# A norm's sum of squares at the head of four layers: other engine, other priority

## The chip, the cores and the metric

One core of a Trainium2 chip runs the whole program. The metric is device time in microseconds, the median of the timed runs. Engines: TensorE (PE, matrix products; PEld, its weight loads), VectorE (DVE), ScalarE (ACT), GpSimd (POOL), and SyncE (SP), which issues most transfers. Engines run beside each other, each takes its own instructions in a fixed order, and semaphores tie them together.

## The reference

The input is 256 tokens of 1024 features. A first block (attention, delta rule, mixture of experts) is followed by a second block of four layers. Only the second block is touched by the change. Cut to what matters:

```python
def rms_norm_2(x, gain):
    y = x * lax.rsqrt(jnp.mean(x * x, axis=-1, keepdims=True) + RMS_EPS) * gain
    return y

for i in range(4):                       # mixers: stick-breaking, conv, gla, stick-breaking
    xn = rms_norm_2(h, norm_gains[i, 0])           # the norm of this document: the mixer's own
    m = mixer(xn, ...)                             # begins with xn @ w_in
    h = h + rms_norm_2(m, norm_gains[i, 1])
    f = squared_relu_mlp(rms_norm_2(h, norm_gains[i, 2]), ffn_w_up[i], ffn_w_down[i])
    h = h + rms_norm_2(f, norm_gains[i, 3])
```

## The kernel before

The residual stream lies transposed in `hT`: eight tiles of 128 features by 256 tokens (all fp32). Weights arrive as 1 MB pieces (`raw`), and `split` (L178) makes two parts of each 128x1024 half: `hi` on ScalarE (L190) and the rest `lo` on VectorE or, for the splits listed in `pool_lo`, on GpSimd (L193). The parts lie in `hi`/`lo`, `mg` or `split` by turns.

A mixer's first product works on `gain * hT`, and the factor `r = rsqrt(mean(hT**2) + eps)`, which belongs to a token and so to a column, is multiplied in later, when a product's result is taken out of PSUM. `operand` (L346) makes the two parts `xh` (ScalarE, L348) and `xl` (VectorE, L349) of `gain * hT` for each of the eight tiles. `chunk` (L221) runs 24 matmuls for 128 output features: `hi` and `lo` against `xh` (L228, L229), then `hi` against `xl` (L231). Its PSUM tile has the tag `g` or `s` by turns, with two buffers each; four chunks can be open before one has to be evacuated. The evacuation (`ev_q`, `ev_k` L676 to L681 in stick-breaking; `ev_c` L514 in conv; `ev_a` L763 in gla) multiplies by `r`.

`r` comes from `factor()` inside `pre` (L363), called by the first evacuation, so in the program it stands behind the first chunk's matmuls. It calls `sumsq` (L314): each hT tile is squared on ScalarE (L324) into `sq` (three buffers; the first of a summed group goes into `ss`); the first `8 - direct` squares are added up in `ss` (L331) by the engine given, and the rest, with `ss`, go through products with a matrix of ones (L337), which add over the partitions into a PSUM tile of tag `s`. Then `Net.factor` (L285) takes logarithm and exponential on ScalarE (L290, L291) and four steps on VectorE (L294 to L297, the last gives `r`).

What comes before: `post` (L380) at the end of a feed-forward layer normalizes its result (three of the eight products `mg` on GpSimd, L395; the others `mh` on VectorE, L398), adds it to hT (L401) and makes the operands tile by tile; `final` (L412) does the same after the first block (L431, L433). Both hold back the splits of the coming weights: four (`post`) or one (`final`) go ahead of the last operand, the others behind it. After `post` splits six and seven of the mixer are subtracted on GpSimd (`pool_lo`).

The order of instructions on each engine comes from a scheduler at build time that takes, among those it holds to be ready, the one with the best priority; priority is the place in the program. `high_priority(offset=50)` moves what it encloses 50 places ahead. The second sum of each layer (`ffn=True`) already uses GpSimd for six squares without that context; it is not changed.

Of the kernel before, what the change touches and what calls it, by code (L numbers as in the profile page):

```python
# [22 lines left out]
D = 1024  # L23
KD = D // P
# [52 lines left out]
class Net:  # L77
# [274 lines left out]
    def pre(self, gain, ffn=False, ops=None):  # L352


        nc = self.nc
        if ops is None:
            ops = self.operands()
            for k in range(KD):
                self.operand(k, gain, *ops)
        xh, xl = ops  # L360
        got = []

        def factor():  # L363
            if not got:
                r = self.nt("r", 2)
                got.append(r)
                if not ffn:
                    with self.tc.high_priority(offset=50):
                        ps = self.sumsq([self.hT[:, k] for k in range(KD)], nc.gpsimd, direct=8)
                        self.factor(ps, D, r)  # L370
                else:
                    ps = self.sumsq([self.hT[:, k] for k in range(KD)], nc.gpsimd, tag="g")
                    v = self.nt("fv", 1)
                    nc.vector.tensor_scalar(out=v, in0=ps, scalar1=1.0 / D, scalar2=EPS, op0=ALU.mult, op1=ALU.add)
                    nc.vector.scalar_tensor_tensor(out=r, in0=v, scalar=8.0 * EPS, in1=v, op0=ALU.mult, op1=ALU.mult)
            return got[0]

        return ([xh[:, k] for k in range(KD)], [xl[:, k] for k in range(KD)]), factor
# [1521 lines left out]
```

## Time and profile before

| | us |
|---|---|
| median of three timed runs | 1939.7 (1937.45 to 1941.39) |
| profiled execution, its own time | 1946.89 |
| its span, first to last instruction | 1945.1 |
| TensorE busy | 1865.7 |
| VectorE busy | 1118.4 |
| ScalarE busy | 952.8 |
| GpSimd busy | 152.5 |

The mean granted clock of TensorE is 0.986 of full speed. Times in the rows below count from the span's start. The four places of the change are the heads of the layers: stick-breaking at about 650 us, conv at 975, gla at 1271, stick-breaking at 1613. A matmul's record overlaps the next, so spacing tells its cost better than its length. A row with "x4" covers four instructions merged into one piece of the timeline, from the first start to the last end; what stands in brackets is the idle time of the engine before it and what ended it.

### The profile page before, as it was taken

Reading aid. Unit: us, or ns where it says so; the run is one execution under the profiler, and the core shown is the slowest. Engines: PE = TensorE matmul, PEld = TensorE weight load, DVE = VectorE, ACT = ScalarE, POOL = GpSimd, SP = SyncE. Lnnn points to the kernel's source line nnn. Section 1 sums busy time; section 2 is a strip of 40 time slices with the busy share of each in tenths; the row PEclk is TensorE's granted clock in tenths of the full one; section 3 lists DMA queues with packets and bytes.
Section 4 is the critical chain, followed back from the end, with each engine's and each line's share of the span. In section 5 each row is a group of like instructions: output and inputs, shape, how many; then the busy total and the mean of one; then the engine's idle time right before and its main releaser. Section 6 shows DMA issues by size and latency. Waiting matters only on the chain.

```text
span 1945.1 us, 34973 instructions
## 1 busy us (share of the span) xinstructions
PE 1865.7 (96%) x14445; PEld 1685.9 (87%) x14445; DVE 1118.4 (57%) x1955; ACT 952.8 (49%) x1742; POOL 152.5 (8%) x162
## 2 busy tenths in 40 slices
PE   6899998998999999999999999989999999999998
PEld 3787788765666899999999999979999998989998
DVE  4848447533332754755586755577675557556554
ACT  4535456322222674544444544455664446645443
POOL 2212111100000000100021100011010001000000
PEclk9999999999999999999999999999999999999999
DMA  9544276588999434455545455523445553335551
GB/s 328 193 152 154 90 239 246 210 324 342 406 399 346 131 130 152 152 174 190 178 145 194 153 183 185 194 87 109 152 152 175 191 177 124 115 131 176 175 192 44
DMA packets 196745, 369.19 MB, mean 190 GB/s; under 512 B 9189, under 2 KB 152997, under 8 KB 185061
## 3 DMA queue, kind: packets, MB, share of 16 engines
q1 hardware_dynamic: 193248, 362.77, 53.5%
q10 hardware_dynamic: 2900, 3.29, 0.5%
q8 instruction: 115, 1.88, 0.4%
q0 software_dynamic: 432, 0.84, 0.2%
q14 instruction: 50, 0.40, 0.1%
HBM read 364.25 MB, written 2.63 MB: 189 GB/s over the span
## 4 chain that ended last, share of the span: by engine, by line
PE 68%; DVE 4%; ACT 3%; POOL 1%; issue 1%; POOLq 0%; DVEq 0%; ACTq 0%
PE g L228 7%; PE g L231 7%; PE g L229 7%; PE big L216 7%; PE big L218 7%; PE big L217 7%; PE g L1761 4%; PE s L1801 2%; PE s L231 2%; PE s L228 2%; PE s L229 2%; PE s L218 1%; PE s L217 1%; PE s L216 1%; POOL ss L331 1%
## 5 line engine op out<-in xcount | busy, mean ns | idle before, releaser
L193 DVE TENSOR_TENSOR lo<-raw,hi 128x1024 fp32r<-128x1024 f32 x304 | 374.8, 1236 | 287.4 <-ACT hi L190 279.8
L190 ACT CAST hi<-raw 128x1024 fp32r<-128x1024 f32 x318 | 330.4, 1043 | 222.1 <-PE s L217 126.3
L228 PE MATMUL g<-xh,hi 128*128 128x256 f32 x1088 | 280.4, 292 | 16.0 <-ACT xh L348 5.6
L229 PE MATMUL g<-xh,lo 128*128 128x256 f32 x1088 | 276.6, 288 | 0.7 <-DVE lo L193 0.7
L228 PEld LDWEIGHTS g<-xh,hi 128*128 128x128 f32 x1088 | 211.2, 194 | 28.2 <-issue 8.4
L229 PEld LDWEIGHTS g<-xh,lo 128*128 128x128 f32 x1088 | 211.5, 194 | 2.2 <-DVE lo L193 0.9
L216 PE MATMUL big<-yh,hi 128*128 128x256 f32 x728 | 206.5, 284 | 0.0
L218 PE MATMUL big<-yh,lo 128*128 128x256 f32 x728 | 206.0, 283 | 0.0
L217 PE MATMUL big<-yl,hi 128*128 128x256 f32 x728 | 206.0, 283 | 0.0
L231 PE MATMUL g<-xl,hi 128*128 128x256 f32 x1088 | 156.7, 286 | 0.0
L231 PEld LDWEIGHTS g<-xl,hi 128*128 128x128 f32 x1088 | 142.7, 194 | 0.4 <-issue 0.2
L216 PEld LDWEIGHTS big<-yh,hi 128*128 128x128 f32 x728 | 139.7, 192 | 0.4 <-issue 0.3
L217 PEld LDWEIGHTS big<-yl,hi 128*128 128x128 f32 x728 | 139.7, 192 | 0.0
L218 PEld LDWEIGHTS big<-yh,lo 128*128 128x128 f32 x728 | 139.7, 192 | 0.0
L449 ACT ACTIVATE sq<-g 128x256 f32<-128x256 f32 x116 | 44.4, 383 | 173.1 <-PE g L231 173.1
L193 DVE TENSOR_TENSOR split<-raw,split 128x1024 fp32r<-128x1024 f32 x64 | 78.3, 1223 | 63.2 <-ACT split L190 63.2
L193 DVE TENSOR_TENSOR mg<-raw,mg 128x1024 fp32r<-128x1024 f32 x64 | 78.2, 1222 | 59.8 <-ACT mg L190 59.7
L190 ACT CAST split<-raw 128x1024 fp32r<-128x1024 f32 x64 | 66.8, 1044 | 63.8 <-PE s L218 42.8
L190 ACT CAST mg<-raw 128x1024 fp32r<-128x1024 f32 x64 | 66.8, 1043 | 51.6 <-PE s L218 36.2
L228 PE MATMUL s<-xh,hi 128*128 128x256 f32 x320 | 85.2, 296 | 5.7 <-DVE fv L294 2.5
L229 PE MATMUL s<-xh,lo 128*128 128x256 f32 x320 | 83.7, 292 | 0.7 <-DVE lo L193 0.7
L271 DVE TENSOR_TENSOR yl<-s,yh 128x256 fp32r<-128x256 f32 x76 | 32.1, 423 | 87.7 <-ACT yh L270 81.3
(613 smaller groups left out, 4665.8 us busy)
## 6 DMA issues: line engine op xcount, KB each, us to landing
raw<-in_ffn_w_up_dram SPq DMA_DIRECT2D x64, 1024.0 KB, 5.4
raw<-in_ffn_w_down_dram SPq DMA_DIRECT2D x64, 1024.0 KB, 5.0
raw<-in_w_mod_dram SPq DMA_DIRECT2D x24, 1024.0 KB, 6.7
raw<-in_sb_w_qkv_dram SPq DMA_DIRECT2D x24, 1024.0 KB, 5.3
raw<-in_w_in_dram SPq DMA_DIRECT2D x22, 1024.0 KB, 7.7
raw<-in_conv_w_in_dram SPq DMA_DIRECT2D x12, 1024.0 KB, 5.3
raw<-in_gla_w_in_dram SPq DMA_DIRECT2D x12, 1024.0 KB, 5.3
extra<-in_w_e_gate_dram SPq DMA_DIRECT2D x11, 1024.0 KB, 9.0
```

The lines of the kernel that those rows point to most:

```text
L190: i = nc.scalar.copy(hi, piece)
L193: j = on.tensor_tensor(out=lo, in0=piece, in1=hi.bitcast(F32), op=ALU.subtract)
L216: a = mm(out, whi, xhi, start=first, stop=False, skip_group_check=skip)
L217: mm(out, whi, xlo, start=False, stop=False, skip_group_check=skip)
L218: mm(out, wlo, xhi, start=False, stop=last, skip_group_check=skip)
L228: mm(ps, hi[:, k, sl], xh[k], start=k == 0, stop=False)
L229: mm(ps, lo[:, k, sl], xh[k], start=False, stop=False)
L231: mm(ps, hi[:, k, sl], xl[k], start=False, stop=k == kn - 1)
L271: self.nc.vector.tensor_tensor(out=lo, in0=src, in1=hi.bitcast(F32), op=ALU.subtract)
L449: nc.scalar.activation(out=t, in_=ps, func=AF.Relu)
L1761: on(mm(gu[i][64 * j:64 * j + 64, :], xg[:, k, o0 + j * cap:o0 + (j + 1) * cap], W[j][k], start=k == 0, stop=k == KD - 1, skip_group_check ...
L1801: on(mm(yps[64 * j:64 * j + 64, :], aT[:, f * P + 64 * j:f * P + 64 * j + 64], W[j][f][:, half * 512:half * 512 + 512], start=f == 0, stop ...
```

## The change

The call of `sumsq` in the mixers' own norm loses its `high_priority` context and its `direct=8`. With the default `direct=2`, six squares are added in `ss` by GpSimd (five additions), and `ss` and the last two squares go through products with ones: three in place of eight. The factor's steps keep their text, and lose the 50 places too. All four mixers use this function.

```diff
                 if not ffn:
-                    with self.tc.high_priority(offset=50):
-                        ps = self.sumsq([self.hT[:, k] for k in range(KD)], nc.gpsimd, direct=8)
-                        self.factor(ps, D, r)
+                    ps = self.sumsq([self.hT[:, k] for k in range(KD)], nc.gpsimd)
+                    self.factor(ps, D, r)
                 else:
```

## Rows read from the trace of the kernel before

**Rows 1.** The page's first part: busy time, share of the span, instructions.
```profile
PE 1865.7 (96%) x14445; PEld 1685.9 (87%) x14445; DVE 1118.4 (57%) x1955; ACT 952.8 (49%) x1742; POOL 152.5 (8%) x162
```

**Rows 2.** TensorE's waits, whole span: us in total, times, longest.
```profile
PE g L228 <- DVE glal L763: 5.2, 1, 5.2
...
PE big L696 <- DVE sbk L681: 1.5, 1, 1.5
...
PE g L228 <- DVE cc L514: 0.6, 1, 0.6
```

**Rows 3.** Timeline of ScalarE, head of conv: start, us, engine, line, operation.
```profile
981.22 0.42 ACT L324 ACTIVATE sq<-hT 128x256 f32<-128x256 f32 x1 [0.27 <-DVE hT L401]
...
982.25 0.49 ACT L348 ACTIVATE xh<-hT,vec_128c 128x256 fp32r<-128x256 f32 x1
982.65 1.03 ACT L190 CAST hi<-raw 128x1024 fp32r<-128x1024 f32 x1
983.59 0.47 ACT L290 ACTIVATE fy<-s,eps 128x256 f32<-128x256 f32 x1
```

**Rows 4.** Timelines of GpSimd and VectorE, conv, behind the operands.
```profile
985.07 4.97 POOL L193 TENSOR_TENSOR lo<-raw,hi 128x1024 fp32r<-128x1024 f32 x2 [8.94 <-ACT hi L190]
...
985.34 2.43 DVE L295 TENSOR_TENSOR fq<-fy 128x256 f32<-128x256 f32 x1
987.81 2.51 DVE L296 SCALAR_TENSOR_TENSOR fq<-fq,fv 128x256 f32<-128x256 f32 x1
990.35 0.43 DVE L297 SCALAR_TENSOR_TENSOR r<-fq,fy 128x256 f32<-128x256 f32 x1
```

**Rows 5.** Timelines of ScalarE and VectorE: split five's cast and `r`, gla, second stick-breaking.
```profile
1278.36 1.03 ACT L190 CAST hi<-raw 128x1024 fp32r<-128x1024 f32 x1
...
1285.94 0.42 DVE L297 SCALAR_TENSOR_TENSOR r<-fq,fy 128x256 f32<-128x256 f32 x1
...
1620.35 1.03 ACT L190 CAST hi<-raw 128x1024 fp32r<-128x1024 f32 x1
...
1628.04 0.42 DVE L297 SCALAR_TENSOR_TENSOR r<-fq,fy 128x256 f32<-128x256 f32 x1
```

**Rows 6.** Timeline of TensorE, head of conv: a chunk's product, products with ones.
```profile
975.61 0.28 PE L228 MATMUL g<-xh,mg 128*128 128x256 f32 x1
...
980.52 1.02 PE L337 MATMUL s<-sq,ones 128*128 128x256 f32 x4
...
982.59 0.59 PE L337 MATMUL s<-sq,ones 128*128 128x256 f32 x2
```

**Rows 7.** GpSimd's five adds, first feed-forward layer (ns min/median/max), and VectorE beside them.
```profile
L331 POOL TENSOR_TENSOR ss<-ss,sq x5: 737/804/1595, 813.1 to 817.4; 128x256 f32<-128x256 f32 x5
...
813.09 5.00 POOL L331 TENSOR_TENSOR ss<-ss,sq 128x256 f32<-128x256 f32 x5 [29.94 <-ACT sq L324]
...
813.35 0.76 DVE L453 TENSOR_TENSOR sq<-sq 128x256 f32<-128x256 f32 x1 [0.54 <-ACT yh L452]
814.15 0.85 DVE L454 TENSOR_TENSOR yl<-sq,yh 128x256 fp32r<-128x256 f32 x1
```

**Rows 8.** Timelines of GpSimd and VectorE, conv, beside the products `mg`.
```profile
973.67 2.46 POOL L395 TENSOR_TENSOR mg<-mg,pr 128x256 f32<-128x256 f32 x3 [155.58 <-DVE pr L297]
...
974.08 0.59 DVE L401 TENSOR_TENSOR hT<-hT,mh 128x256 f32<-128x256 f32 x1
...
975.47 0.95 DVE L349 SCALAR_TENSOR_TENSOR xl<-hT,vec_128c,xh 128x256 fp32r<-128x256 f32 x1
```

**Rows 9.** Timelines of VectorE and TensorE, first stick-breaking layer.
```profile
662.51 0.41 DVE L297 SCALAR_TENSOR_TENSOR r<-fq,fy 128x256 f32<-128x256 f32 x1
...
664.64 0.41 DVE L681 TENSOR_TENSOR sbk<-g,r 128x256 f32<-128x256 f32 x1
...
666.94 0.70 PE L696 MATMUL big<-sbq,sbk 64*128 64x256 f32 x4
```

**Rows 10.** Stretch after gla's wait: length, busy by engine, granted clock, DMA share, GB/s.
```profile
1287.00:1294.00 7.00, 6.96 (x26) 4.93 (x27) 2.64 (x4) 2.57 (x4) 0.00 (x0) 0.60 0.46 148
```

## The prediction

> **What bounds the kernel now.** I read the page first: TensorE is busy for 96% of the span [rows 1], so only what moves TensorE moves the time. The norm that changes is computed four times, once at the head of each layer of the second block. The next view is the list of what TensorE waited for. Three of the four heads show there: the gla layer (5.2 us for `glal`), the second stick-breaking layer (1.5 us for `sbk`), the conv layer (0.6 us for `cc`) [rows 2]. All three releasers are the first evacuations that multiply by the norm's factor `r`. So there TensorE has nothing left to do when `r` comes, and `r` sets the end. The first stick-breaking layer is not in that list: its TensorE runs through.
>
> Then I went back from `r` in the timelines. In the conv layer ScalarE ends the last operand `xh` (982.25), then casts split five (`hi`, 982.65), then takes the logarithm `fy` of the sum (983.59) without idling [rows 3]: the sum is ready just in time. GpSimd subtracts splits six and seven from 985.07 for 4.97 us, and the two small VectorE steps L295 and L296, of 0.43 us by the like step L297, take 2.43 and 2.51: each ends just after a GpSimd subtraction does [rows 4]. `r` is ready at 990.78, 8.1 us after split five's cast began. In the gla layer it is 1278.36 to 1286.36, 8.0 us; in the second stick-breaking layer 1620.35 to 1628.46, 8.1 [rows 5]. So in three layers `r` hangs on the moment when ScalarE is through with the eight operands, plus a fixed 8.1 us of which about 4 are GpSimd holding VectorE up.
>
> **What is removed.** Five of eight products with ones go. Two records of such a product take 0.59, four take 1.02, so a record adds 0.215 and a product 0.43 [rows 6]; 5 x 0.43 = 2.15 us of TensorE a head, 8.6 in all. In the three layers where TensorE waits for `r` at the end, this work lies ahead of that wait: the wait grows by 2.15 and the time doesn't change. I cost it at nothing there; were that cover gone, it would be worth the 2.15. The last product still needs the last square, so the sum isn't ready earlier.
>
> **What is moved.** The squares (ScalarE), the adds, the products and the six steps of the factor lose their head start of 50 places. It issues no DMA, so SP's queue isn't passed. The order on an engine is not the program's: a product of chunk three (weights in `mg`) runs at 975.61, before chunk one is through [rows 6]. So I expect the squares to go on filling ScalarE's gaps between two operands, but behind an operand that is ready as well. Now a square is in front: ScalarE idles 0.27 at 981.22 for that square's hT, with two operands queued behind it [rows 3]. That wait goes: -0.3 a head. The factor's steps stay ahead of split three and later in the program, as now. The GpSimd queue gets five adds between the three products `mg` (done 976.13) and splits six and seven; with the adds done by then, those splits aren't held up.
>
> **What is added.** Five adds on GpSimd a head. The same five exist in the feed-forward layers: 0.80 us each in the median, 5.00 for the five together [rows 7], against 8.9 us of empty GpSimd between 976.1 and 985.1 [rows 4, 8]: they fit. Two costs stay.
> First, ScalarE: `sq` has three buffers, so the last square waits for the fourth add. Squares come as hT does, and GpSimd keeps that pace except at the end: +0.3 a head.
> Second, VectorE: it makes hT and `xl` in just this stretch, in steps of about 0.43. How much an add delays them no row of this place shows, so I bound it. During the three `mg` products (2.46 us) L401 took 0.59 and L349 0.95: 0.16 + 0.52 = 0.7 lost, 0.28 per us of GpSimd [rows 8]. During the five adds in a feed-forward layer L453 and L454 took 0.76 and 0.85, 0.75 lost in 5.0, 0.15 per us [rows 7], with VectorE mostly idle. L295 and L296 were stopped for the whole rest of a GpSimd operation: 1.0 per us [rows 4]. The lower end is 0, if every add falls where VectorE reads PSUM or waits. I take 0.28, the row with the same VectorE steps. Four of the five adds come before the last hT: 4 x 0.80 x 0.28 = 0.9 a head; bounds 0 and 3.2.
> The Trainium skill, page "SBUF — State Buffer", section "SBUF: two separate sides", says that VectorE operations with two SBUF inputs and GpSimd share one port pair as an exclusive lock, and that the loser stops entirely; this speaks against the change. L295 and L296 agree with it; L401 at 974.08, begun inside a product of 0.82 and only 0.16 longer, lost less than the whole. By the page alone the sum would be that of the full stop, below; by the row it is the one here.
>
> **The sum.** Three layers: -0.3 + 0.3 + 0.9 = +0.9 us until split five's cast may start, so `r` and TensorE come 0.9 later: +2.7. Bounds per layer: -0.6 (no delay by the port, the ScalarE wait gone, and 0.3 more because the logarithm no longer sits before split six's cast) and +2.9 (each add stops VectorE fully, less 0.3 for a PSUM step beside it): -1.8 and +8.7 together.
> First stick-breaking layer: TensorE isn't in the list of waits for `r`. `r` is ready at 662.92, the first pair of evacuations it needs at 665.05, TensorE takes them at 666.94 [rows 9]: a slack of 1.9 us. I expect `r` about 1 later, which that slack hides, and the first chunk up to 1 earlier, since products no longer stand between its matmuls, less the same 0.9 by the port: -0.3, bounds -1.5 and +2.
> Sum +2.4 us. The profiled execution lasts 1946.89 us, 1.8 of it outside its span and 7.2 above the median of the three timed runs; a change of 2.4 is carried over to the median unscaled: 1939.7 + 2.4 = **1942.1 us**, from 1936.4 (-3.3) to 1950.4 (+10.7) by the bounds. No clock cost is in the sum: after the 5.2 us wait in the gla layer the granted clock averages 0.60 over 7.0 us, which is 5.6 us at 1.2 GHz [rows 10]; a wait of 1.5 + 2.15 + 0.9 = 4.5 us in the second stick-breaking layer might do the same, up to +2.8. It belongs to the upper part of the range. What a measurement of this kernel can tell from no change is about 0.2%, 3.9 us.
>
> **Rivals.**
> *Full stop at the port* (slower). Each add holds VectorE up for its whole length wherever a step with two SBUF operands is next; L295 and L296 speak for it, L401 against. From an average loss of 0.45 us per us of add on, it is over the bound. At 2.9 a layer less nothing at the first: +8.7, about 1948.4. By the Trainium skill, "SBUF — State Buffer", "SBUF: two separate sides", this would be the outcome; the rows bear it out in part, so it has a chance of its own.
> *The squares really come behind* (slower). If ScalarE's order puts the eight squares behind the last operand, the chain is 0.4 + 5.0 of adds + 1.3 of products after it, where now the sum ends 0.4 behind it. Splits six and seven then queue behind the adds on GpSimd. The factor takes two ScalarE steps of 0.47 and four VectorE steps of 0.43, 2.6 in all [rows 3, 4], and up to 2.5 behind one such split: `r` would come 6.7 + 2.6 + 2.5 = 11.8 us after the last operand in place of 8.0; with the operands some 0.8 earlier, +3.0 a layer, and at the first layer the slack of 1.9 is used up, +1.0: +10, about 1949.7. Against it stands that ScalarE has gaps between operands now (0.27 at 981.22 is one).
> *Nothing moves the end.* The 8.1 us fixed behind split five absorb a sum that is up to 2 us late, since L295 waits for GpSimd anyway; with the adds beside PSUM steps the time stays at 1939.7. This is also the case where the order on the engines hardly changes, and the edit does less than it says.
> *A gain.* The lower bounds together: 3 x -0.6 and -1.5 to -2.15 at the first layer, some -4: 1935.7. All of the 8.6 us (1931.1) would need `r` earlier in three layers, which no row supports.
>
> **How the numbers follow.** The forecast's case 0.40 (its own range 1939.5 to 1945, of which 0.30 lies within 0.2% and 0.10 above); full stop 0.17; squares behind 0.15; nothing moves 0.15; gain 0.13, of which 0.08 beyond 0.2%. So faster 0.08, same 0.30 + 0.15 + 0.05 = 0.50, slower 0.10 + 0.17 + 0.15 = 0.42. The range 1936 to 1950 holds the forecast's case, no change, and most of the three others.
>
> **What would show it.** Products: L337 with six records a head in place of sixteen, and TensorE's waits for `glal`, `sbk` and `cc` longer by about 2.15 + 0.9. The squares still between operands on ScalarE, the last one or two behind the last operand. GpSimd adds between `mg` and splits six and seven; L401 and L349 longer in that stretch by about 0.9 us in all. `r` still about 8 us after split five's cast. The prediction is wrong if `r` moves against that cast, if the squares stand in a block behind the operands, or if the waits of TensorE at the three heads shrink.

## The result, and the profile after

The changed kernel takes 1955.3 us (median of four runs, 1952.2 to 1957.1) against 1938.8 before (1937.5 to 1941.4; four runs, of which the 1939.7 of the prediction had three): a ratio of 1.0081, 95% interval 1.0066 to 1.0096, or +16.5 us. The forecast was +2.4, and its range ended at 1950.

TensorE does less and GpSimd more, as written: 40 matmul records fewer, 20 us of adds more; the span grows all the same. First part of the page of the kernel after, then TensorE's waits there (us in total, times, longest), which answer to [rows 1, 2]:

```profile
PE 1864.8 (95%) x14405; PEld 1684.3 (86%) x14405; DVE 1119.8 (57%) x1955; ACT 954.0 (49%) x1742; POOL 172.7 (9%) x182
```

```profile
PE s L337 <- POOL ss L331: 5.8, 4, 2.7
PE g L228 <- DVE glal L762: 5.5, 1, 5.5
...
PE big L695 <- DVE sbk L680: 2.2, 1, 2.2
```

The first line is new: at each head the first product with ones waits for GpSimd's sum. The waits for `glal` and `sbk` have hardly grown, so most of the loss lies ahead of them.

**Where it was lost.** The two profiled executions can't be compared from their start: before the first head their code is alike, and the traces of this study reach that head anywhere between 640.5 and 650.8 us. So I measure each head with its layer, from its first operand product to that of the next head (the last one to the span's end):

| us, from head to head | stick-breaking | conv | gla | stick-breaking | sum |
|---|---|---|---|---|---|
| before | 324.5 | 296.0 | 342.0 | 331.8 | 1294.3 |
| after | 329.6 | 299.8 | 345.9 | 334.1 | 1309.4 |
| difference | +5.1 | +3.9 | +3.9 | +2.3 | +15.1 |

That is nearly all of the 16.5. A head is read from one execution, so its tenths are rough: in the runs below that leave a head's code as it was, it differs from before by up to 0.7. Now the conv head, the like of which is found in gla. VectorE and GpSimd of the kernel after (start, us):

```profile
979.84 3.71 POOL L331 TENSOR_TENSOR ss<-ss,sq 128x256 f32<-128x256 f32 x4 [2.30 <-ACT sq L324]
...
980.66 1.43 DVE L349 SCALAR_TENSOR_TENSOR xl<-hT,vec_128c,xh 128x256 fp32r<-128x256 f32 x2
982.02 0.94 DVE L400 TENSOR_TENSOR hT<-hT,mh 128x256 f32<-128x256 f32 x1
982.88 0.94 DVE L400 TENSOR_TENSOR hT<-hT,mg 128x256 f32<-128x256 f32 x1
```

Four of the five adds come as one train, and VectorE's steps that meet it take 0.94 in place of 0.41 to 0.44: one VectorE step for each add, by turns. From the first operand product (975.27 before, 975.56 after) split five's cast now starts 9.33 us later, in place of 7.38 [rows 3]: +1.95 (gla +2.20, the last head +2.25, from the same rows of those heads and [rows 5]). Next, TensorE and ScalarE of the kernel after:

```profile
978.75 0.58 PE L228 MATMUL g<-xh,hi 128*128 128x256 f32 x1 [1.59 <-ACT xh L348]
...
983.60 1.22 PE L337 MATMUL s<-ss,ones 128*128 128x256 f32 x2 [0.92 <-POOL ss L331]
...
986.11 1.90 PE L231 MATMUL g<-xl,hi 128*128 128x256 f32 x8
987.82 1.05 PE L337 MATMUL s<-sq,ones 128*128 128x256 f32 x4
...
984.89 1.98 ACT L190 CAST hi<-raw 128x1024 fp32r<-128x1024 f32 x2
988.91 0.47 ACT L290 ACTIVATE fy<-s,eps 128x256 f32<-128x256 f32 x1 [2.05 <-PE s L337]
```

TensorE waits 1.59 for an operand, where before it had products with ones to do, and from there on its matmuls stand 0.21 apart in place of 0.12. Then it stands 0.92 before the sum, in its fixed order, and the last products come at 987.82, behind a block of chunk one that takes 1.90. ScalarE has waited 2.05 for them when it takes the logarithm; before, it came to it without idling [rows 3]. Stretches of the kernel after, conv and gla, then the first head (us, busy by engine, granted clock, DMA share, GB/s; one layout for all such rows):

```profile
978.50:988.50 10.00, 8.83 (x37) 8.21 (x38) 7.43 (x13) 6.24 (x14) 5.03 (x5) 0.53 0.00 1
1278.50:1288.50 10.00, 9.00 (x36) 8.27 (x37) 7.26 (x13) 6.07 (x14) 5.49 (x5) 0.51 0.04 3
...
650.30:660.30 10.00, 7.34 (x34) 6.82 (x34) 5.25 (x7) 7.30 (x14) 4.58 (x5) 0.68 0.39 117
```

The like stretch of conv before:

```profile
978.21:988.21 10.00, 9.97 (x72) 9.38 (x73) 8.73 (x16) 8.44 (x17) 3.14 (x2) 1.00 0.00 1
```

The granted clock is at its lower level, 1.2 GHz, for nearly all of the first two stretches; in the first ten microseconds of the same heads before it was 1.00. In the last head of the kernel after it stays 1.00. At the end of the conv chain, VectorE's `cc` before, and then VectorE of the kernel after, which answers to [rows 4]:

```profile
991.34 0.42 DVE L514 TENSOR_TENSOR cc<-g,cr 128x256 f32<-128x256 f32 x1
```

```profile
990.67 2.42 DVE L295 TENSOR_TENSOR fq<-fy 128x256 f32<-128x256 f32 x1 [0.82 <-ACT fy L291]
993.12 0.42 DVE L296 SCALAR_TENSOR_TENSOR fq<-fq,fv 128x256 f32<-128x256 f32 x1
993.58 0.43 DVE L297 SCALAR_TENSOR_TENSOR r<-fq,fy 128x256 f32<-128x256 f32 x1
994.04 0.42 DVE L505 TENSOR_TENSOR cr<-r 128x256 f32<-128x256 f32 x1
994.38 1.22 DVE L193 TENSOR_TENSOR lo<-raw,hi 128x1024 fp32r<-128x1024 f32 x1
995.52 0.42 DVE L513 TENSOR_TENSOR cc<-g,cr 128x256 f32<-128x256 f32 x1
```

`r` is ready 9.1 us after split five's cast (8.1 before), and a subtraction of 1.22 now stands between `cr` and `cc`; before, `cc` ended 0.98 after `r`, now 1.93. So conv loses 1.95 + 1.0 + 0.95 = 3.9, what the table says.

In the first head the picture is another. ScalarE and TensorE of the kernel after:

```profile
650.14 1.01 ACT L324 ACTIVATE sq<-hT 128x256 f32<-128x256 f32 x3
652.34 0.42 ACT L324 ACTIVATE sq<-hT 128x256 f32<-128x256 f32 x1 [1.19 <-POOL ss L331]
...
655.07 1.03 ACT L190 CAST mg<-raw 128x1024 fp32r<-128x1024 f32 x1
...
649.18 0.38 PE L228 MATMUL g<-xh,hi 128*128 128x256 f32 x1 [1.67 <-ACT xh L348]
655.57 0.70 PE L337 MATMUL s<-ss,ones 128*128 128x256 f32 x2 [2.66 <-POOL ss L331]
```

All eight squares stand behind the last operand, wait for a free `sq`, that is for GpSimd, and hold splits three and four up behind them. The adds come behind VectorE's steps here and stretch none of them. TensorE waits 1.67 for an operand, where before a product with ones filled the time, and 2.66 for the sum. The stretch at clock 0.68 costs some 10 x 0.32 = 3.2 more, and five products save 2.15: 1.67 + 2.66 + 3.2 - 2.15 = 5.4, measured 5.1. This adds up where the time went; it doesn't say what each cause alone would cost, for a slower TensorE shortens a wait behind it. `r` plays no part here: it is ready at 662.5 and TensorE takes its first use at 667.2.

### The profile page after: what moved, and what is told of

It is laid out like the page before. It is cut to its first block, busy times and chain, and to the rows that moved or that the text cites. A ratio compares the mean times of both kernels' runs of the same rounds, so it can differ in the third digit from the quotient of the medians.

```text
span 1955.4 us, 34909 instructions
## 1 busy us (share of the span) xinstructions
PE 1864.8 (95%) x14405; PEld 1684.3 (86%) x14405; DVE 1119.8 (57%) x1955; ACT 954.0 (49%) x1742; POOL 172.7 (9%) x182
## 3 DMA queue, kind: packets, MB, share of 16 engines
HBM read 364.25 MB, written 2.63 MB: 188 GB/s over the span
## 4 chain that ended last, share of the span: by engine, by line
PE 53%; issue 6%; ACT 3%; DVE 3%; POOL 1%; POOLq 0%; DVEq 0%
PE g L231 6%; PE g L228 6%; PE big L216 6%; PE g L229 6%; PE big L218 6%; PE big L217 6%; PE s L231 2%; PE s L228 2%; PE s L229 2%; POOL ss L331 1%; PE s L337 1%; PE s L218 1%; PE s L217 1%; PE s L216 1%; ACT sbs L702 1%
```

## The experiments

The theory that I went on with: adds on GpSimd stop VectorE nearly for their length, and fewer products that wait in order let TensorE's clock fall. The rival: the lost head start does it. Differences from head to head, worked out as in the table above:

| us against before | time (median) | ratio, 95% interval | heads 1, 2, 3, 4 | sum |
|---|---|---|---|---|
| order alone (e1) | 1946.0 | 1.0023 to 1.0046 | +3.1, +3.0, +1.0, -0.1 | +6.9 |
| adds, order kept (e2) | 1949.5 | 1.0038 to 1.0072 | +3.7, +1.7, +2.7, +3.7 | +11.8 |
| five idle adds (e3) | 1948.6 | 1.0033 to 1.0067 | +1.5, +1.0, +0.9, +1.6 | +5.0 |
| adds on VectorE (e4) | 1946.4 | 1.0027 to 1.0051 | +2.1, +1.4, +1.5, +1.4 | +6.4 |
| three products, no adds (e5) | 1948.0 | 1.0030 to 1.0059 | +0.7, +1.7, +1.0, +0.9 | +4.4 |
| after, TensorE filled (e6) | 1952.6 | 1.0062 to 1.0095 | +4.8, +3.6, +2.4, +2.3 | +13.1 |
| three heads alone (e7) | 1947.3 | 1.0032 to 1.0065 | +0.1, +2.6, +3.9, +3.2 | +9.8 |
| before, no GpSimd split (e8) | 1935.9 | 0.9971 to 0.9991 | 0.0, -0.2, -1.8, -1.6 | -3.6 |
| first head alone (e9) | 1943.9 | 1.0004 to 1.0033 | +5.2, -0.3, -0.7, 0.0 | +4.2 |
| ten idle adds (e10) | 1954.3 | 1.0043 to 1.0090 | +3.2, +2.7, +2.9, +5.3 | +14.1 |
| after, no GpSimd split (e11) | 1953.1 | 1.0040 to 1.0078 | +5.1, +3.9, +2.7, -0.5 | +11.2 |
| e8, and `r` first (e12) | 1933.6 | 0.9946 to 0.9974 | 0.0, -0.8, -5.0, -1.6 | -7.4 |

Before beside these runs: 1938.8 (e1 to e4), 1938.5 (e5 to e8), 1939.4 (e9 to e12). The sums of the heads are from one execution each, and lie up to 5 us from the differences of the medians (most in e3 and e5).

**e1, the order alone.**

```diff
 (after)
-                    ps = self.sumsq([...], nc.gpsimd)
+                    ps = self.sumsq([...], nc.gpsimd, direct=8)
```

> The priority is taken off, but all eight squares go to eight products with ones and GpSimd adds nothing: the order alone. If the adds and the missing products make the loss (my theory now), the time stays within 4 us of the kernel before (1935 to 1943 against 1938.8), and GpSimd is still free in the four heads. If the order alone makes the loss (rival), most of the 16.5 us is here: 1950 or more, with the squares in a block behind the operands in the first stick-breaking layer.

+7.2 lies between the two times expected. The factor's last step begins 14.75 to 14.9 after the first operand product in the last three heads, as before (14.7 to 15.1), so the head start was worth nothing for `r` there. What it did hold is what comes next. VectorE of e1 in conv:

```profile
988.29 0.42 DVE L297 SCALAR_TENSOR_TENSOR r<-fq,fy 128x256 f32<-128x256 f32 x1
988.63 1.22 DVE L193 TENSOR_TENSOR lo<-raw,hi 128x1024 fp32r<-128x1024 f32 x1
989.76 0.42 DVE L505 TENSOR_TENSOR cr<-r 128x256 f32<-128x256 f32 x1
990.10 1.22 DVE L193 TENSOR_TENSOR mg<-raw,mg 128x1024 fp32r<-128x1024 f32 x1
991.24 0.42 DVE L513 TENSOR_TENSOR cc<-g,cr 128x256 f32<-128x256 f32 x1
```

Two subtractions have slipped in between `r` and `cc`; TensorE waits 2.63 for `cc` in place of 0.58. In the first head it waits 1.67 for an operand and the clock averages 0.83 over the first 10 us: 1.67 + 1.7 = 3.4, measured 3.1.

**e2, the adds alone.**

```diff
 (before)
-                        ps = self.sumsq([...], nc.gpsimd, direct=8)
+                        ps = self.sumsq([...], nc.gpsimd)
```

> The 50 places of head start stay, but six squares are added on GpSimd and three products remain: the adds and the fewer products without the change of order. If they make the loss, 1948 to 1955 (three layers of 3 to 4 us, the first layer less than its 5.0 because its squares come early). If the order makes it, within 4 us of the kernel before.

+10.6, as expected if the adds and the fewer products make the loss; they are the larger half. With the order kept, split five's cast starts 9.1 after the first operand product in the last three heads, nearly as late as in the kernel after (9.3), so the delay of the operands doesn't need the lost head start. e1 and e2 together make 17.8 where both edits made 16.5.

**e3 and e10, the port alone.**

```diff
 (before; e10: each k twice)
                         ps = self.sumsq([...], nc.gpsimd, direct=8)
                         self.factor(ps, D, r)
+                        for k in range(1, 6):
+                            junk = self.nt("ss", 1)
+                            nc.gpsimd.tensor_tensor(out=junk, in0=self.hT[:, k], in1=self.hT[:, k - 1], op=ALU.add)
```

> The kernel before, with five further adds on GpSimd, of hT[k] and hT[k-1] for k of 1 to 5, into a scratch tile that nothing reads: the port alone, with no wait of TensorE behind it and all eight products left. If an add stops VectorE's steps with two operands in SBUF nearly for its whole length, as the stretched steps of the changed kernel say (2.0 to 2.2 us a head), the three layers lose 2 to 2.2 each and the time is 6 to 7 us above the kernel before (1945 to 1946). If the recorded 0.9 a head was right, +2.7 (1941.5). If the port costs nothing and the loss is all in the wait for the sum, 1939.

> The kernel before with ten scratch adds a head in place of five, again read by nothing. Five put r 0.99 to 1.29 us later in the conv, gla and last heads, by about one VectorE step of 0.41 stretched to 0.95 for each add that meets one. If the loss goes by the time that GpSimd is at it, r comes 2 to 3.5 later than before in these heads and the heads lose about twice the 4.8 of five adds: 1946 to 1952. If VectorE loses only where a train of adds meets the last steps of hT, not more than 1 us beyond the run with five.

GpSimd, VectorE and ScalarE of e3 in conv, where the first operand product is at 970.33; then the same of e10, first operand product at 972.64 (L404 is hT's add, L401 the product `mh` that reads PSUM):

```profile
975.25 1.64 POOL L372 TENSOR_TENSOR ss<-hT 128x256 f32<-128x256 f32 x2 [0.76 <-DVE hT L404]
976.24 0.95 DVE L404 TENSOR_TENSOR hT<-hT,mh 128x256 f32<-128x256 f32 x1
978.70 1.03 ACT L190 CAST hi<-raw 128x1024 fp32r<-128x1024 f32 x1
```

```profile
975.68 6.87 POOL L372 TENSOR_TENSOR ss<-hT 128x256 f32<-128x256 f32 x8 [0.42 <-DVE hT L404]
978.41 0.94 DVE L404 TENSOR_TENSOR hT<-hT,mg 128x256 f32<-128x256 f32 x1
979.27 0.47 DVE L401 SCALAR_TENSOR_TENSOR mh<-big,vec_128c,pr 128x256 f32<-128x256 f32 x1
980.15 0.94 DVE L404 TENSOR_TENSOR hT<-hT,mh 128x256 f32<-128x256 f32 x1
982.77 1.03 ACT L190 CAST hi<-raw 128x1024 fp32r<-128x1024 f32 x1
```

Split five's cast starts 8.37 after the first operand product in e3 (+0.99 against before; +1.27 in gla and the last head) and 10.13 in e10 (+2.75; +3.87 and +3.04). Twice the adds cost 2.4 to 3.1 times as much here, so the price doesn't go by GpSimd's time. It goes by the meetings: each VectorE step with two SBUF operands that comes due as an add begins loses some 0.53 (0.94 for 0.41), and there are two such steps beside the adds of e3 in conv and seven beside those of e10. The step L401, with one operand in PSUM, loses nothing in the middle of the train (0.47 as ever). Neither expectation came out whole: e3's time lies above all that was expected, though its cast lies nearer to the recorded 0.9 than to 2.0; e10's heads, expected at about twice those of e3 or hardly more, lose 14.1 against 5.0. The Trainium skill, "SBUF — State Buffer", section "SBUF: two separate sides", says of this port pair that whoever starts first has it for the whole instruction and the other blocks; the rows of 0.94 agree (each of these steps ends some 0.3 us after the add that it met), and the row of 0.47 with its limit to VectorE operations that read two SBUF operands. Open is that e3's median lies 9.8 above before while its profiled execution, the shortest of its four (1945.5), shows 5.0 in the heads; what the others lost beyond it no trace shows.

**e4, the adds on VectorE.**

```diff
 (after)
-                    ps = self.sumsq([...], nc.gpsimd)
+                    ps = self.sumsq([...], nc.vector)
```

> The changed kernel with its five adds on VectorE instead of GpSimd: three products, same order, no sharing with GpSimd. An add then costs VectorE some 0.43 us (its like steps), 2.2 a head for five, about what the port takes now, but the sum needs less time from the last square on. If the wait for GpSimd's slow sum and the port make the loss, 1945 to 1950. If TensorE's clock after five missing products makes it, 1953 to 1957 as now, with a granted clock near 0.5 in the conv and gla heads.

1946.4, within the expected range: the five adds cost less on VectorE itself than on GpSimd. Split five's cast is on time again (7.13 after the first operand product in the last three heads, before 7.10 to 7.38). The sum is late instead: `r` is ready 10.0 to 11.3 us behind that cast.

**e5 and e6, three products without adds, and the changed kernel with TensorE filled.**

```diff
 (after, e5: in sumsq, five squares are made and not used)
-            else:
+            elif add:
                 (eng or nc.vector).tensor_tensor(out=ss, in0=ss, in1=sq, op=ALU.add)
 (after, e6: in sumsq, with fill = xh0 to xh4)
+        for t in fill:
+            mm(ps, self.ones, t, start=True, stop=True)
         for i, t in enumerate(terms):
```

> The changed kernel without its adds: all eight squares are made, five of them go nowhere, three products with ones remain, and no sum is added on GpSimd or VectorE. Left out of the computation: the sum lacks five of its eight terms. It is the order and the missing products, without port and without a wait for a sum. If order (+7.2 in the run with all eight products) and adds are all there is, 1944 to 1948. If TensorE with fewer products falls to 1.2 GHz by itself, the conv and gla heads show a granted clock near 0.5 here too and the time is 1949 to 1953. If the products' own work counts for something, 1938 to 1942.

> The changed kernel with five more products, of ones with the finished operands xh0 to xh4, into the same PSUM tile ahead of the three real ones: TensorE has its old eight products again, and nothing waits for the new ones. If the half clock of the changed kernel in the first, conv and gla heads is the cause of a part of the loss, the granted clock there comes back to 1.00 and the time falls by 2 to 5 us, to 1950 to 1953. If the clock costs nothing (r hangs on VectorE and GpSimd alone), 1954 to 1957.

The first ten microseconds of the conv head in e5, then in e6:

```profile
969.89:979.89 10.00, 8.95 (x63) 8.19 (x64) 8.50 (x20) 8.11 (x19) 1.36 (x2) 1.00 0.00 1
```

```profile
970.38:980.38 10.00, 7.95 (x52) 7.23 (x53) 9.15 (x18) 6.31 (x16) 5.06 (x6) 1.00 0.00 1
```

e5 keeps its clock there with three products, in gla too: it isn't the missing products alone that let it fall. Nor is it the adds alone: e3 and e10, with adds and all eight products, keep 1.00 through the first 14 us of every head. In conv and gla it is these together, with the waits that the adds bring. In the first head the order is enough: e1, with eight products and no adds, waits 1.67 there and falls for 3.4 us. e5's time is at the upper edge of what was expected, and its profile shows 4.4. e6 has the same adds and split five's cast as late as after (9.34), but the clock is back at 1.00, and `r` is ready 7.9 us after that cast in place of 9.1 (gla 7.7 in place of 9.2). TensorE's wait of 1.59 is 0.64 here in conv, with products of xh in it.

A second comparison needs no added products: the conv head of e7 has the text, the adds and the wait (1.58) of the kernel after. Its stretch, in the place of the 978.50 row above:

```profile
968.73:978.73 10.00, 8.73 (x52) 8.20 (x53) 7.85 (x14) 7.78 (x17) 5.32 (x5) 0.83 0.00 1
```

With the clock at 0.83 in place of 0.53, `r` is ready 7.9 us after the cast, as in e6, and the head loses 2.6 in place of 3.9 (one subtraction stands ahead of `cc` in both). So the clock is what made the 1.0 to 1.2 in conv and gla between cast and `r`. How much of it reaches the time depends on what follows: e6 gains 1.5 over after in gla, but 0.2 in conv, where two subtractions of 1.22 stand between `r` and `cc` in place of one. By the heads e6 wins 2.0 over after, by the medians 2.7; the intervals overlap, so its size is less sure than its being there. In the first head it wins only 0.3: the sum is waited for 3.22 there, and the clock still falls, later, for 3.4 us. That is 3.22 + 1.7 = 4.9, measured 4.8.

**e7 and e9, three heads alone, the first alone.** In both a counter in `pre` picks the form of the head.

> The change in the conv, gla and second stick-breaking heads alone; the first stick-breaking head as before. By the heads of the two traces the first head loses 5.0 us of some 15: so 1949 to 1952 here (16.5 less 5.0, give or take 1.5). If the first head still has the slack that the prediction gave it, 1954 to 1956.

> The change in the first stick-breaking head alone, the other three as before. By the heads of the profiles it loses 5.0 us there, by the difference of the run with the three other heads 16.5 - 8.9 = 7.6: so 1943.5 to 1946. If the heads don't add up (the first head's loss was a chance of the clock), 1938 to 1941.

+8.9, below the expected 1949 to 1952, and +4.5, within what was expected. Together they are 13.4 of 16.5: the heads add up to about their sum, and the first loses its 5 us by itself. Two heads of e7 differ from the same heads of the kernel after, conv by -1.3 and the last by +1.0; the clock goes with both. In conv it is at the lower level for 3.4 us in place of 10.2, in the last head for 3.4 us from 21.0 after the first operand product, where after has no fall.

**e8, e11 and e12, GpSimd's splits.** Where two subtractions on GpSimd hold L295 and L296 up [rows 4], the same port is at work.

```diff
 (e8: before, e11: after)
-        self.nsplit, self.pool_lo = 0, (6, 7) if after and len(after) == 1 else ()
+        self.nsplit, self.pool_lo = 0, ()
 (e12: e8, and in split; self.late is the last step of the factor, in the three heads)
+        if self.late and self.nsplit in (6, 7, 8):
+            self.after(j, self.late)
```

> The kernel before, with splits six and seven subtracted on VectorE and not on GpSimd in the three heads. In the trace of before L295 and L296 end just after a GpSimd subtraction does, 2.43 and 2.51 for steps of 0.43. If that is the port, both take 0.43 here, r comes up to 4 us sooner against split five's cast (some 4 to 6 in place of 8.1), and 2.4 us of VectorE (two steps of 1.22) go behind it: 1933 to 1938 if what follows r waits for TensorE alone, 1938 to 1941 if the two subtractions on VectorE take the place of the gain.

> The changed kernel with splits six and seven subtracted on VectorE in the three heads. Without GpSimd's splits L295 and L296 don't stop for them (the same edit gave the kernel before 1.0 us a head in r and -2.6 in the time). If the late sum alone sets r, it gains as much: 1951 to 1954. If the changed kernel's adds and splits on GpSimd queue behind one another and that is a part of the loss, more: 1945 to 1950.

> The kernel before with no split on GpSimd in the three heads, and the subtractions of splits six to eight held on VectorE until r is made (an order on one engine, without a wait). In the run with GpSimd's splits moved, four subtractions of 1.22 stood between the steps of the factor: r can come 2.4 to 3.6 us sooner than there. In the conv and last heads TensorE hardly waits for r any more, so nothing is left to gain; in the gla head it waited 4.2: 1932 to 1935 if that gain is kept, 1936 if the later splits take it back.

VectorE in conv, of e8 and then of e12 (L297 there is L295 of before):

```profile
984.09 0.42 DVE L295 TENSOR_TENSOR fq<-fy 128x256 f32<-128x256 f32 x1
984.42 1.22 DVE L193 TENSOR_TENSOR lo<-raw,hi 128x1024 fp32r<-128x1024 f32 x1
985.56 0.42 DVE L296 SCALAR_TENSOR_TENSOR fq<-fq,fv 128x256 f32<-128x256 f32 x1
```

```profile
981.15 0.43 DVE L297 TENSOR_TENSOR fq<-fy 128x256 f32<-128x256 f32 x1
981.61 0.43 DVE L298 SCALAR_TENSOR_TENSOR fq<-fq,fv 128x256 f32<-128x256 f32 x1
982.07 0.42 DVE L299 SCALAR_TENSOR_TENSOR r<-fq,fy 128x256 f32<-128x256 f32 x1
982.41 1.22 DVE L193 TENSOR_TENSOR lo<-raw,hi 128x1024 fp32r<-128x1024 f32 x1
```

In e8 L295 and L296 take 0.42, but subtractions of 1.22 stand between them and `r` gains only 1.0 a head: -2.6. In e12 these are held behind `r`, whose step begins 4.0 to 4.1 sooner than before in each of the three heads (10.7 to 11.0 after the first operand product): -5.8 in all, most of it in gla (-5.0). TensorE's wait for `glal` shrinks from 5.2 to 2.2, with one of 0.7 behind it. The rest goes with the clock, which stays at 1.00 behind the shorter wait, where it averaged 0.60 before [rows 10]. The like stretch of e12:

```profile
1279.00:1286.00 7.00, 6.34 (x40) 5.17 (x41) 4.08 (x5) 3.52 (x5) 0.00 (x0) 1.00 0.71 223
```

Before, TensorE worked 5.6 us at the lower level there, which costs 2.8; with 2.4 less of waits that makes 5.2, measured 5.0. e12 beats both kernels, by a ratio of 0.9960 to before. e8, e11 and e12 came out as expected in their times, though `r` gained less in e8 than the 4 us that the port alone would have given. The changed kernel gains 2.2 by the medians from the edit of e8 (that is e11), within its spread.

## Why the prediction was wrong, by its own steps

- **Bound by `r` in three heads, 8.1 us behind split five's cast.** Right as a picture: the losses of conv and gla add up along that chain, and e12, which cuts it, gains. But the "fixed" 8.1 wasn't: it was 9.1 in conv and 9.2 in gla, where the clock fell, and 7.9 in the last head, where it didn't, though TensorE waited longer for the sum there (1.30 against 0.92).
- **Products removed: nothing gained.** Right, L337 has six records a head and no head is faster. Wrong is that they cost nothing: they were also what TensorE did while it waited for operands, and the three left wait in its fixed order for GpSimd, 0.9 to 2.7 a head. The sign that was named, waits for `glal`, `sbk` and `cc` longer by 2.15 + 0.9, didn't come (+0.3, +0.7 and -0.2): TensorE came to them late itself.
- **Squares between operands; -0.3 and +0.3.** Right for three heads, where the wait moved rather than went: in e1 the last operand comes 0.3 to 0.6 sooner, but two squares stand behind it, and the cast comes no sooner (7.44 against 7.10 to 7.38). Wrong in the first head, where they stand in a block. The argument from a product of chunk three ahead of chunk one [rows 6] showed that the order may differ from the program's, not which order it will be; each head came out by itself.
- **The adds on VectorE, 0.9 a head.** The term was mis-sized: the cast came 1.95, 2.20 and 2.25 later, of which 1.9 in each head is against e1, which has the order and no adds. So the adds cost VectorE 1.9 a head, twice the term. The rate of 0.28 per us of GpSimd was read where PSUM steps stood between [rows 8]; e3, whose adds are spread, measured 0.99 to 1.27, close to it. The step that failed is the assumption that the five adds meet VectorE as the three products did. The squares come in pairs, so four adds make a train, on just the steps that finish hT.
- **First head, -0.3.** It missed by most: +5.1. I had priced `r` against its slack of 1.9 [rows 9]; that slack held (`sbk` is ready at 664.86 now and taken at 667.20), and TensorE itself ran late.
- **Clock at nothing.** The fall was named for the last head, where it didn't come; it came in the other three. In conv and gla it put `r` 1.0 to 1.2 later against the cast (e6, and e7 in conv), in the first head TensorE lost some 3.2 by the stretch at 0.68.
- **The factor's steps stay ahead of split three and later.** Wrong: one subtraction slipped ahead of `cc` or `glal` in the kernel after, two ahead of `cc` in e1, some 1 us each.

The terms were +0.9 a head for three and -0.3; they measured +3.9, +3.9, +2.3 and +5.1. Of the rivals, the full stop at the port named the mechanism and its sign (1.9 of its 2.9 a head), but that is 5.7 of 15. The squares behind came true in the first head alone. No rival held several of them at once, so the range ended at 1950.

## What to carry to other kernels

Before work goes from a busy engine to GpSimd, look at when its pieces come due, and at which VectorE steps with two SBUF operands stand there: count the meetings, not the mean rate. Work on TensorE that "costs nothing" ahead of a wait may be what fills its gaps; ask what its queue then waits for and what clock it comes back at. And a head start given to a chain also orders what follows it: compare the whole queue behind the chain's end, not the chain alone.

## What the runs showed of the hardware

A GpSimd add of about 0.8 us and a VectorE add of 0.41, both on SBUF, ran by turns, 0.94 for each VectorE step, for as long as the train lasted (eight adds in 6.87 us), while VectorE's step with an operand in PSUM took its usual 0.47 in between. In the kernel after, TensorE waited 1.50 and 1.59 for operands at the heads of conv and gla, and the granted clock went to its lower level; at the last head it waited 1.50 and 1.36, and the clock stayed at 1.00. The same went together in the first 19 us of these heads in e2, e7 and e11 (1.57 to 1.59 in conv and gla, 1.35 to 1.36 in the last head), but the fall lasted between 3.4 and 10.2 us. The length of a wait doesn't decide alone: in e4 the clock fell in conv 1.0 us after the first operand product, behind the wait of 1.50 and ahead of the next, of 0.88, and stayed through the first 17 us of gla, with waits of 1.50, 1.26, 0.65 and 0.64. What decides stays open; a loss of this kind can come or stay away between heads that are nearly alike. Five products on operands that are finished (e6) kept the clock at 1.00 through the first ten microseconds of conv and gla.
